# A two-block network on one core: norm weights moved from the rows to the transposed side, and the rms factor to what follows the projections

## Chip, core and metric

One Trainium2 core runs the whole kernel in one launch. The metric is the device time of one execution in microseconds (us). PE is the matrix engine, DVE the vector engine, ACT the scalar engine, POOL the GpSimd engine; SP only starts weight loads.

## What is computed

256 tokens of width 2048 pass through a first block (four branches merged by gates, an out-projection and a layer norm) and then a second one (an rms norm, a projection into a state-space group and a forget-gate attention, an out-projection, and a layer that selects among 16384 experts). What lies between the two blocks, and what reads it, is this:

```python
def layer_norm(x, g, b):
    ...
    y = (xf - mu) * lax.rsqrt(var + LN_EPS) * g.astype(jnp.float32) + b.astype(jnp.float32)
    return y.astype(x.dtype)

def first_block(x, w_in, ...):
        ...
        out = jnp.einsum('bsd,de->bse', merged, w_out[l])
        x = layer_norm(ALPHA * x + out, ln_g[l], ln_b[l])

def rmsnorm(x, w):
    xf = x.astype(jnp.float32)
    xf = xf * lax.rsqrt(jnp.mean(xf * xf, axis=-1, keepdims=True) + EPS)
    return (xf * w.astype(jnp.float32)).astype(x.dtype)

def second_block(x, ln1_w, w_in, ...):
        h = rmsnorm(x, ln1_w)
        proj = h @ w_in
        z, xbc, dt_raw, q, k, v, f_raw = jnp.split(proj, split_at, axis=-1)
        y_ssd = ssd_group(z, xbc, dt_raw, ...)
        y_fox = fox_group(q, k, v, f_raw, fox_f_bias)
        x = x + jnp.concatenate([y_ssd, y_fox], axis=-1) @ w_out
        x = x + peer(rmsnorm(x, ln2_w), peer_wq, peer_k1, peer_k2, peer_u, peer_v)
```

The layer norm's result is needed twice: normed, as the input of block 2's projection, and as it is, as the residual to which block 2's out-projection is added.

## The kernel before

**The stream.** All weights pass through as chunks of 128 x 2048 (1 MB), loaded by SP into three buffers `wr`. Each chunk is used in two halves of 128 x 1024. ACT casts a half into a rounded high part `wh`, DVE subtracts to get the low part `wl`, and there are four buffers of each. PE multiplies three times per 128 rows of the contraction: high part of the activations by `wh`, low part by `wh`, high part by `wl`. The activations stand transposed (width on partitions, tokens along the free side) in `XH` (high) and `XL` (low). `N_chunk` makes an output with tokens on partitions, by matmuls of 512 columns, six for each half and each token half t = 0, 1; `T_chunk` makes an output with tokens along the free side, by matmuls of 256 columns, 24 for each half.

**Order.** Each engine executes what the program wrote for it, in that order; there is no dynamic scheduling. The loop at the end of `_kern` walks over the halves. `catch` writes the cast and the subtraction of the halves up to three ahead (`LOOK`), then the half's matmuls are written, and after its first few matmuls `bg()` writes steps of background tasks (generators in four lanes). Which task steps come where is set by estimated clocks in `Tasks` and `Meter`, at build time. A task step that one engine has to wait for is therefore a wait for all that the same engine has behind it.

**The boundary between the blocks.** The rows `X[0]`, `X[1]` (128 tokens x 2048 each) hold block 1's sum. `state["tail"](t)` evicts the last 512 columns of the out-projection into them; `ln_stats` makes mean and standard deviation of the rows. Then `ln_part` and `ln_last` apply the layer norm in pieces of 128 x 512, with `lng` and `lnb`, the weights and offsets broadcast over all partitions, which were loaded into the buffers `GC` and `CV` during block 1; ACT squares the pieces and sums them, `rms_diag` makes a 128 x 128 diagonal matrix of 1/rms, and `to_T` multiplies pieces of X by it on PE, which transposes and scales at once (16 matmuls for each t), evicts with the rms norm's weight `ln1_w` to `XH` on ACT and `XL` on DVE. POOL takes the last piece of the layer norm and four `wl` subtractions.

PE's stream goes on meanwhile where it can. The first four chunks of block 2's `w_in2` (96 matmuls of 512 columns, for half of the attention's V) stand in the boundary: `N_chunk(..., lead=boundary1b)` writes the token half t = 0 of the first two chunks (24 matmuls), then calls `boundary1b`, which transposes t = 1, and writes the led t = 1 matmuls after it. Next come one chunk with 32 matmuls for dt and the forget gate (`dtf_chunk`; it has one cast, a small subtraction `wh<-wr,wh` and no `wl` for each half) and twelve `T_chunk`s for the state-space group's input (`ev_xbc` into `PX`). `ev_dtf` evicts the dtf output to `LS`, and `tr`, written two background points later, transposes it back by two PE instructions `pm<-cst,LS` in the middle of the second half of the first xbc chunk.

Of the kernel before, what the change touches and what calls it, by code (L numbers as in the profile page):

```python
# [16 lines left out]
P = 128  # L17
D = 2048
# [15 lines left out]
for _name, _w in (("pool_scale", 8), ("conv_w", 31 * 8), ("conv_b", 8), ("conv_g", 8), ("conv_lb", 8),  # L34
                  ("conv2_w", 48), ("conv2_b", 12), ("ln1_w", 16), ("ln2_w", 16), ("ssd_norm", 8)):
    PAR[_name] = (_n, _w)
    _n += _w
# [181 lines left out]
def _kern(tc, nc, ctx, A, out):  # L219
# [125 lines left out]
    def N_chunk(kq, evac, korder=(0, 1, 2, 3), hold=False, lead=None, slot=0):  # L345
        def fn(half, hi, lo):
# [456 lines left out]
    for br, (_, need, ysrc) in enumerate(order):  # L803
# [4 lines left out]
        for jj in range(8):  # L808
            def pre_y(need=need, ysrc=ysrc, br=br):
                flush()  # L810
                tasks.require(*need)
                if br == 0:
                    tasks.require("pool")
                split_Y(ysrc)
                if br == 2:
                    nc.gpsimd.dma_start(X[0], A["xN"][0])
                    nc.gpsimd.dma_start(X[1], A["xN"][1])
                    nc.gpsimd.dma_start(GC.rearrange("p j t -> p (j t)"), row_ap("ln_g"))
                if br == 3:
                    nc.gpsimd.dma_start(CV.rearrange("p j t -> p (j t)"), row_ap("ln_b"))  # L820
# [29 lines left out]
    def warm():  # L850
        SC.activation(small[:, 63:64], eps5, AF.Sqrt)

# [9 lines left out]
    diag = [per.tile([P, P], F32, name=f"diag{t}") for t in range(2)]  # L862
# [20 lines left out]
    lnb = CV.rearrange("p j t -> p (j t)")  # L883
    lng = GC.rearrange("p j t -> p (j t)")

# [8 lines left out]
    def ln_last(t):  # L894
        rs = small[:, 6 + t:7 + t]
        s = slice(1536, 2048)
        SC.activation(X[t][:, s], X[t][:, s], AF.Identity, bias=small[:, 8 + t:9 + t], scale=rs)
        G.tensor_tensor(X[t][:, s], X[t][:, s], lng[:, s], op=OP.mult)
        G.tensor_tensor(X[t][:, s], X[t][:, s], lnb[:, s], op=OP.add)

    def ln_part(t, hooks=()):
        mv = small[:, 2 * t:2 * t + 2]
        rs = small[:, 6 + t:7 + t]
        for h in (0, 1, 3, 2):
            s = slice(h * 512, (h + 1) * 512)
            if h < 3:
                V.scalar_tensor_tensor(X[t][:, s], X[t][:, s], mv[:, 0:1], lng[:, s], op0=OP.subtract, op1=OP.mult)
                V.scalar_tensor_tensor(X[t][:, s], X[t][:, s], rs, lnb[:, s], op0=OP.mult, op1=OP.add)
            SC.activation(VQ[:, s], X[t][:, s], AF.Square, accum_out=small[:, 16 + 4 * t + h:17 + 4 * t + h])
            if h < len(hooks):  # L910
                hooks[h]()
# [5 lines left out]
    def boundary1():  # L917
        flush()
        hc = tasks.now
        state["tail"](0)  # L920
        ln_stats(0)
        ln_last(0)
        ln_part(0, [lambda: catch(hc, G), lambda: catch(hc + 1, G)])
        state["tail"](1)
        rms_diag(0, sum_sq(0))
        ln_stats(1)
        to_T(0, "ln1_w", {2: lambda: catch(hc + 2, G), 6: lambda: catch(hc + 3, G), 10: lambda: ln_last(1)})
        ln_part(1)
        rms_diag(1, sum_sq(1))

    def boundary1b():
        to_T(1, "ln1_w")
        state["hold"] = False
        p1.close()
        block2()
# [5 lines left out]
    def block2():  # L941
# [36 lines left out]
        b2["sel"] = a2.tile([P, 32], BF, name="sel")  # L978
        V.memset(b2["c4"][:, :, 3], 0.0)
        with nc.allow_low_precision(reason="sums of an identity's entries"):  # L980
            V.tensor_reduce(b2["sel"], ident.rearrange("p (a h) -> p h a", a=4), axis=AX.X, op=OP.add)
        tasks.add("dt", dt_gen)
# [9 lines left out]

    def ev_dtf(o):
# [3 lines left out]
        def tr():  # L997
# [4 lines left out]
            V.tensor_tensor(b2["dtf"], p4[:, :, 0], b2["fb"][:, None, :].to_broadcast([P, 2, 32]), op=OP.add)  # L1002
            V.tensor_tensor(b2["dtf"], p4[:, :, 1], b2["dtf"], op=OP.add)
# [221 lines left out]
    def ev_k2(j):  # L1225
        def f(o):
            SC.copy(b2["K2"][:, j % 2], o)
            flags["k2"] = j + 1
        return f

    def ev_z(n):
        def f(t, ps):
            s = b2["w"].tile([P, 512], F32, name="t2")
            SC.activation(s, ps, AF.Sigmoid)
            V.tensor_tensor(b2["ZN"][:, t, n * 512:(n + 1) * 512], ps, s, op=OP.mult)
# [3 lines left out]
    def ev_vf(n):  # L1239
        def f(t, ps):  # L1240
            SC.copy(b2["VN"][:, t, n * 512:(n + 1) * 512], ps)
        return f

    def fox_gen(j):
        def make(ln):
# [18 lines left out]
            for blk in range(2):  # L1264
# [8 lines left out]
                for i in (1, 0):  # L1273
                    V.scalar_tensor_tensor(L[:, i, :nk], ps[i][:, :nk], 0.125,
# [33 lines left out]
               pres=[boundary1] + [None] * 3)  # L1308
# [425 lines left out]
def layout(inputs):  # L1734
# [56 lines left out]
    def tp(v):  # L1791
# [5 lines left out]
                                  tp(f["ssd_norm_w_2"])], axis=1)  # L1797
# [49 lines left out]
```

## Time and profile before

| what | value |
| --- | --- |
| median of 3 runs | 3078.73 us (3076.59 to 3081.01) |
| the profiled execution's own time | 3082.12 us |
| its span, first to last instruction | 3080.4 us |
| granted TensorE clock, mean over the span | 0.996 |
| PE busy | 3031.5 us (98%) |
| DVE, ACT, POOL busy | 2202.0, 1575.4, 214.6 us |

All times inside the kernel are those of one profiled execution, counted from its span's start. The boundary lies at 1112 to 1169 us of it, and block 2's projections and mixers end near 1460 us. A granted clock of 1.00 is 2.4 GHz, one of 0.50 is 1.2 GHz.

### The profile page before, as it was taken

To read this page: it belongs to the slowest core of one execution; us is meant where nothing else is said; L and a number is where in the kernel's file an instruction comes from. 1 tells how busy PE (TensorE), PEld (TensorE's weight loads), DVE (VectorE), ACT (ScalarE), POOL (GpSimd) and SP (SyncE) were. 2 spreads that over 40 slices of the span, in tenths; PEclk is the share of its full clock that TensorE was granted. 3 is DMA by queue.
4 is the path that set the end of the run, shared out by engine and by line. 5 is a ranking of instruction groups with operands and counts; after the bars stand their busy time and mean duration, and the time that the engine had idled before them with its cause. 6 is when DMAs were issued, how large, how long until landed. Compare 5 with 4: busy or idle time off the path is not lost.

```text
span 3080.4 us, 53114 instructions
## 1 busy us (share of the span) xinstructions
PE 3031.5 (98%) x21972; PEld 2829.0 (92%) x21972; DVE 2202.0 (71%) x3195; ACT 1575.4 (51%) x2199; POOL 214.6 (7%) x187
## 2 busy tenths in 40 slices
PE   8999999999999989999999999999999999999998
PEld 8899999999999869897799999999999888888887
DVE  7888866555555667665589989779796666666665
ACT  4443566444444445566444467667675444444444
POOL 0000000000000020100000012223131000000000
PEclk9999999999999999999999999999999999999999
DMA  7555455555555535433445565675658766666654
GB/s 267 193 185 192 177 199 180 210 196 209 192 205 193 192 127 187 165 137 137 178 178 192 207 218 208 244 264 213 248 194 344 269 245 221 247 251 250 240 212 150
DMA packets 92227, 640.61 MB, mean 208 GB/s; under 512 B 10273, under 2 KB 10449, under 8 KB 17745
## 3 DMA queue, kind: packets, MB, share of 16 engines
q1 hardware_dynamic: 78192, 559.06, 50.4%
q0 software_dynamic: 13504, 77.63, 6.9%
q8 instruction: 172, 2.82, 0.4%
q14 instruction: 71, 0.57, 0.1%
q10 hardware_dynamic: 288, 0.52, 0.0%
HBM read 601.53 MB, written 35.65 MB: 207 GB/s over the span
## 4 chain that ended last, share of the span: by engine, by line
PE 96%; DVE 1%; ACT 1%; issue 1%; DMA 0%; POOL 0%; SPq 0%; DVEq 0%; ACTq 0%
PE pm L208 92%; PE bg L208 4%; ACT wh L208 1%; DVE wl L208 0%; DMA wr<-w_in 0%; DVE X L208 0%; DVE XL L208 0%; POOL keys L1531 0%; DVE stg L208 0%; DVE gb L208 0%; ACT XH L208 0%; DVE PX L208 0%; ACT PX L208 0%; ACT keys L208 0%; SPq L433 0%
## 5 line engine op out<-in xcount | busy, mean ns | idle before, releaser
L208 DVE TENSOR_TENSOR wl<-wr,wh 128x1024 fp32r<-128x1024 f32 x1048 | 1292.4, 1236 | 804.6 <-ACT wh L208 799.5
L208 ACT CAST wh<-wr 128x1024 fp32r<-128x1024 f32 x1054 | 1109.2, 1053 | 1364.4 <-PE pm L208 1307.5
L208 PE MATMUL pm<-XH,wh 128*128 128x256 f32 x4976 | 1388.9, 279 | 8.0 <-ACT wh L208 8.0
L208 PE MATMUL pm<-XL,wh 128*128 128x256 f32 x4976 | 1379.0, 277 | 0.0
L208 PE MATMUL pm<-XH,wl 128*128 128x256 f32 x4960 | 1375.6, 277 | 1.1 <-DVE wl L208 1.1
L208 PEld LDWEIGHTS pm<-XH,wh 128*128 128x128 f32 x4976 | 936.2, 188 | 14.2 <-ACT wh L208 8.0
L208 PEld LDWEIGHTS pm<-XL,wh 128*128 128x128 f32 x4976 | 936.9, 188 | 1.0 <-issue 0.7
L208 PEld LDWEIGHTS pm<-XH,wl 128*128 128x128 f32 x4960 | 933.6, 188 | 1.6 <-DVE wl L208 1.6
L208 PE MATMUL pm<-wh,whl 128*128 128x512 f32 x1024 | 398.3, 389 | 0.0
L208 PE MATMUL pm<-wh,whh 128*128 128x512 f32 x1024 | 398.3, 389 | 0.0
L208 PE MATMUL pm<-wl,whh 128*128 128x512 f32 x1024 | 398.3, 389 | 0.0
L208 PEld LDWEIGHTS pm<-wl,whh 128*128 128x128 f32 x1024 | 192.3, 188 | 39.9
L208 PEld LDWEIGHTS pm<-wh,whh 128*128 128x128 f32 x1024 | 192.3, 188 | 39.8
L208 PEld LDWEIGHTS pm<-wh,whl 128*128 128x128 f32 x1024 | 192.3, 188 | 39.8
L208 PE MATMUL pm<-wh,XH 128*128 128x512 f32 x448 | 177.7, 397 | 3.7 <-ACT XH L208 3.7
L208 PE MATMUL pm<-wh,XL 128*128 128x512 f32 x448 | 176.8, 395 | 0.7 <-DVE XL L208 0.7
L208 PE MATMUL pm<-wl,XH 128*128 128x512 f32 x448 | 176.2, 393 | 0.0
L208 PE MATMUL pm<-YH,wh 128*128 128x256 f32 x512 | 141.9, 277 | 0.0
L1531 POOL TENSOR_TENSOR keys<-cst,t 128x512 f32<-128x512 f32 x64 | 126.9, 1983 | 211.2 <-ACT ga L208 211.0
L208 PE MATMUL pm<-YL,wh 128*128 128x256 f32 x512 | 141.5, 276 | 0.0
L208 PE MATMUL pm<-YH,wl 128*128 128x256 f32 x512 | 141.5, 276 | 0.0
L208 DVE SCALAR_TENSOR_TENSOR CV<-R,par,CV 128x256 f32<-128x256 f32 x240 | 116.2, 484 | 7.3
(292 smaller groups left out, 2368.5 us busy)
## 6 DMA issues: line engine op xcount, KB each, us to landing
wr<-w_in SPq DMA_DIRECT2D x190, 1024.0 KB, 4.8
wr<-uT SPq DMA_DIRECT2D x128, 1024.0 KB, 4.9
wr<-v SPq DMA_DIRECT2D x128, 1024.0 KB, 4.8
wr<-w_branch SPq DMA_DIRECT2D x32, 1024.0 KB, 4.8
wr<-w_out SPq DMA_DIRECT2D x32, 1024.0 KB, 4.8
wr<-wq SPq DMA_DIRECT2D x16, 1024.0 KB, 4.8
Ad<-ast POOLq DMA_DIRECT2D x16, 1024.0 KB, 5.1
Gd<-stg POOLq DMA_DIRECT2D x16, 1024.0 KB, 10.2
```

The source lines that it names most:

```text
L208: return f(out, *a, **k)
L1531: G.tensor_tensor(x, it, t3[:, 0, n0:n0 + 4, None].to_broadcast([P, 4, P]), op=OP.subtract)
```

## The change

The rows are only centred and scaled by the layer norm's mean and deviation (`normal`, on DVE or ACT). `turn` transposes a 128 x 512 piece on PE with the identity and evicts it on ACT with a scale and a bias per partition: `ln_g*ln1_w` and `ln_b*ln1_w`, which are made beforehand in `gb_w`; the result, in `VQ`, is rounded to `XH` and subtracted to `XL`. What is now multiplied by `w_in2` lacks the factor 1/rms of each token. A new background task, `resid`, makes the layer norm's true rows (times `ln_g`, plus `ln_b`), their squares, 1/rms as a column `rr` and, by one PE product of ones with diagonals, as a matrix `Rr` with tokens along the free side. Each eviction of block 2's projections multiplies by one of them; `tr` requires that `resid` is finished. The two broadcast rows are loaded no longer in block 1 but by POOL at the end of the boundary, into block 2's buffers `ZN` and `YF`. The diff, cut:

```diff
@@ N_chunk
                 if len(led) == 4:
-                    lead()
-                    for a in led:
+                    lead(-1)
+                    for n, a in enumerate(led):
                         part(*a)
+                        lead(n)
...
-                nc.gpsimd.dma_start(GC.rearrange("p j t -> p (j t)"), row_ap("ln_g"))
-                if br == 3:
-                    nc.gpsimd.dma_start(CV.rearrange("p j t -> p (j t)"), row_ap("ln_b"))
...
+        V.tensor_tensor(gb_w[:, 0], pv("ln_gT", 0, 16), pv("ln1_w", 0, 16), op=OP.mult)
+        V.tensor_tensor(gb_w[:, 1], pv("ln_bT", 0, 16), pv("ln1_w", 0, 16), op=OP.mult)
...
+    def normal(t, h, act=False):
+        x = X[t][:, h * 512:(h + 1) * 512]
+        rs = small[:, 6 + t:7 + t]
+        if act:
+            SC.activation(x, x, AF.Identity, bias=small[:, 8 + t:9 + t], scale=rs)
+        else:
+            V.tensor_scalar(x, x, small[:, 2 * t:2 * t + 1], rs, op0=OP.subtract, op1=OP.mult)
+    def turn(t, h, act=False):
...
+            PE.transpose(p[:, i * P:(i + 1) * P], X[t][:, k * P:(k + 1) * P], ident)
...
+            SC.activation(u[:, i * P:(i + 1) * P], p[:, i * P:(i + 1) * P], AF.Identity,
+                          bias=gb_w[:, 1, k:k + 1], scale=gb_w[:, 0, k:k + 1])
...
+        if act:
+            SC.copy(hs, u)
+        else:
+            V.tensor_copy(hs, u)
+        V.tensor_sub(XL[:, 4 * h:4 * h + 4, t * P:(t + 1) * P], u, hs.bitcast(F32))
@@ boundary1
-        ln_last(0)
-        ln_part(0, [lambda: catch(hc, G), lambda: catch(hc + 1, G)])
+        normal(0, 0)
+        normal(0, 1)
+        catch(hc)
+        turn(0, 0)
+        catch(hc + 1)
+        turn(0, 1, True)
         state["tail"](1)
-        rms_diag(0, sum_sq(0))
         ln_stats(1)
-        to_T(0, "ln1_w", {2: lambda: catch(hc + 2, G), 6: lambda: catch(hc + 3, G), 10: lambda: ln_last(1)})
-        ln_part(1)
-        rms_diag(1, sum_sq(1))
...
+    def boundary1b(n):
+        hc = tasks.now
+        if n < 0:
+            turn(1, 1, True)
+            normal(0, 2)
+            normal(0, 3)
+        elif n == 0:
+            turn(0, 2)
+            normal(1, 2)
+        elif n == 1:
+            catch(hc + 1)
+            turn(1, 2)
+            normal(1, 3)
+        elif n == 2:
+            catch(hc + 2)
+            turn(0, 3)
+        else:
+            turn(1, 3)
+            state["hold"] = False
+            p1.close()
+            block2()
@@ block2
+        nc.gpsimd.dma_start(b2["ZN"].rearrange("p t c -> p (t c)"), row_ap("ln_g"))
+        nc.gpsimd.dma_start(b2["YF"].rearrange("p j t -> p (j t)"), row_ap("ln_b"))
+    def resid_gen(ln):
...
+                V.tensor_tensor(X[t][:, s], X[t][:, s], g[:, s], op=OP.mult)
+                V.tensor_tensor(X[t][:, s], X[t][:, s], b[:, s], op=OP.add)
...
+                SC.activation(junk, X[t][:, s], AF.Square, accum_out=small[:, 16 + 4 * t + h:17 + 4 * t + h])
...
+            SC.activation(small[:, 10 + t:11 + t], sum_sq(t), AF.Sqrt, bias=eps6, scale=1.0 / D)
...
+        V.reciprocal(rr[:, :2], small[:, 10:12])
+        V.tensor_scalar(rr[:, 2:], rr[:, :2], 0.125, None, op0=OP.mult)
...
+            V.tensor_scalar(diag[t], ident, rr[:, t:t + 1], None, op0=OP.mult)
...
+            PE.matmul(p[:, t * P:(t + 1) * P], ones, diag[t], start=True, stop=True)
+        SC.copy(b2["Rr"], p[:, :S])
...
+            V.tensor_scalar(b2["VN"][:, t, :512], b2["VN"][:, t, :512], rr[:, t:t + 1], None, op0=OP.mult)
@@ ev_dtf, tr
-            V.tensor_tensor(b2["dtf"], p4[:, :, 0], b2["fb"][:, None, :].to_broadcast([P, 2, 32]), op=OP.add)
-            V.tensor_tensor(b2["dtf"], p4[:, :, 1], b2["dtf"], op=OP.add)
+            tasks.require("resid")
+            for c in range(2):
+                for i in range(2):
+                    V.scalar_tensor_tensor(b2["dtf"][:, c], p4[:, c, i], b2["rr"][:, c:c + 1],
+                                           b2["dtf"][:, c] if i else b2["fb"], op0=OP.mult, op1=OP.add)
@@ ev_xbc; ev_k2 likewise
-            SC.copy(b2["PX"][:, j, 3:], o)
+            V.tensor_tensor(b2["PX"][:, j, 3:], o, b2["Rr"], op=OP.mult)
...
-               pres=[boundary1] + [None] * 3)
+               pres=[(boundary1, boundary1_1), (boundary1_2, boundary1_3), None, None])
```

What is left out of it: `boundary1_1` to `boundary1_3` write two splits, `normal(1, 0)` and `normal(1, 1)` on ACT, and `turn(1, 0)`; the scales at the evictions of z, the second V half and the attention's scores take `rr` as an operand that the instruction already had room for.

The first place is DVE's order from the last `XL` of the boundary on. `wl<-wr,wh` and `wh<-wr,wh` are the stream's subtractions, X are the rows. Before:

```order
L208 MEMSET c_12620 128x2x32
L208 TENSOR_REDUCE sel<-cst 128x32
L208 TENSOR_TENSOR wl<-wr,wh 128x1024 x4
L208 TENSOR_TENSOR wh<-wr,wh 128x8x32 x2
L208 TENSOR_TENSOR wl<-wr,wh 128x1024 x5
L208 TENSOR_TENSOR dtf<-pm,fb 128x64
L208 TENSOR_TENSOR dtf<-pm,dtf 128x64
L208 TENSOR_TENSOR wl<-wr,wh 128x1024
```

And now, in the same place:

```order
L209 MEMSET c_12604 128x2x32
L209 TENSOR_REDUCE sel<-cst 128x32
L209 TENSOR_TENSOR wl<-wr,wh 128x1024 x2
L209 TENSOR_TENSOR wh<-wr,wh 128x8x32
L209 TENSOR_TENSOR X_76<-X_76,ZN 128x512
L209 TENSOR_TENSOR X_76<-X_76,YF 128x512
L209 TENSOR_TENSOR X_76<-X_76,ZN 128x512
L209 TENSOR_TENSOR X_76<-X_76,YF 128x512
L209 TENSOR_TENSOR wh<-wr,wh 128x8x32
L209 TENSOR_TENSOR wl<-wr,wh 128x1024 x2
L209 TENSOR_TENSOR X_76<-X_76,ZN 128x512
L209 TENSOR_TENSOR X_76<-X_76,YF 128x512
```

Products and sums of the rows now stand between the stream's subtractions; ten more of them, three `wl`, and the small steps to `rr`, `diag` and `VN` follow before the four steps that make `dtf`. So 16 operations on X with six of the stream's subtractions (the second `wh`, and five `wl`) lie between the arrival of `ZN` and the diagonal.

The second place is PE's order in the second half of the first xbc chunk, around the transposes of dtf (`pm<-cst,LS`). Before:

```order
L208 MATMUL pm<-XH,wl 128x256
L208 MATMUL pm<-cst,LS_12609 128x64 x2
L208 MATMUL pm<-XH,wh 128x256
L208 MATMUL pm<-XL,wh 128x256
L208 MATMUL pm<-XH,wl 128x256
```

And now:

```order
L209 MATMUL pm<-XH,wl 128x256
L209 MATMUL pm<-cst,LS_12593 128x64 x2
L209 MATMUL bg_12817<-diag,cst 128x128 x2
L209 MATMUL pm<-XH,wh 128x256
L209 MATMUL pm<-XL,wh 128x256
```

The two products with `diag` (fp32, into a bank `bg`) are new here, in front of the stream's next matmul; in both programs 161 stream matmuls stand between the out-projection's last one and this place (96 of `w_in2`'s first four chunks, 32 of dtf and 33 of xbc).

The third place is POOL's queue at the end of the boundary, with `fb`, `ea`, `ds` as small constants of block 2. Before:

```order
L898 TENSOR_TENSOR X_76<-X_76,GC 128x512
L899 TENSOR_TENSOR X_76<-X_76,CV 128x512
L297 TENSOR_TENSOR wl<-wr,wh 128x1024 x4
L898 TENSOR_TENSOR X_77<-X_77,GC 128x512
L899 TENSOR_TENSOR X_77<-X_77,CV 128x512
L970 DMA fb<-rows 128x32
L971 DMA ea<-rows 128x16
L972 DMA ds<-rows 128x16
L973 MEMSET PX 128x12x3
```

And now:

```order
L819 DMA X_77<-xN 128x2048
L1006 DMA fb<-rows 128x32
L1007 DMA ea<-rows 128x16
L1008 DMA ds<-rows 128x16
L1009 MEMSET PX 128x12x3
L1017 DMA ZN<-rows 128x2048
L1018 DMA YF<-rows 128x2048
```

POOL has no arithmetic left in the boundary, and two loads of 1 MB stand behind the small ones, whose first is held until the boundary's buffers are free.

## Rows read from the trace of the kernel before

**Rows 1.** Page: busy time of each engine, and the chain that ended last.
```profile
PE 3031.5 (98%) x21972; PEld 2829.0 (92%) x21972; DVE 2202.0 (71%) x3195; ACT 1575.4 (51%) x2199; POOL 214.6 (7%) x187
...
PE 96%; DVE 1%; ACT 1%; issue 1%; DMA 0%; POOL 0%; SPq 0%; DVEq 0%; ACTq 0%
```

**Rows 2.** Timeline of PE, 1108 to 1172: start, length, tile, idle before and releaser.
```profile
1112.09 0.39 PE L208 MATMUL pm<-wh,XL 128*128 128x512 f32 x1
1112.32 0.40 PE L208 MATMUL pm<-wl,XH 128*128 128x512 f32 x1
1122.34 4.46 PE L208 MATMUL bg<-diag,X 128*128 128x128 f32 x24 [9.63 <-issue]
1127.30 1.14 PE L208 MATMUL bg<-diag,X 128*128 128x128 f32 x8 [0.50 <-DVE XL L208]
...
1139.13 5.75 PE L208 MATMUL bg<-diag,X 128*128 128x128 f32 x32 [5.17 <-DVE diag L208]
...
1161.22 0.28 PE L208 MATMUL pm<-XH,wh 128*128 128x256 f32 x1
...
1168.96 0.39 PE L208 MATMUL pm<-XH,wh 128*128 128x256 f32 x1
```

**Rows 3.** Grouped instructions by form, 1106 to 1460: count; busy us, mean ns; idle before.
```profile
L208 DVE TENSOR_TENSOR wl<-wr,wh 128x1024 fp32r<-128x1024 f32 x93 | 113.6, 1224 | 92.3 <-ACT wh L208 88.4 <-PE bg L208 3.8
L208 ACT CAST wh<-wr 128x1024 fp32r<-128x1024 f32 x99 | 103.8, 1050 | 103.3 <-PE pm L208 82.2 <-issue 17.6 <-ACT LS L208 1.8
...
L208 ACT ACTIVATE VQ<-X 128x512 f32<-128x512 f32 x8 | 5.0, 627 | 10.1 <-DVE X L208 10.0
...
L208 DVE TENSOR_TENSOR XS<-XS,LS 128x256 f32<-128x256 f32 x12 | 4.9, 419 | 0.0
...
L208 ACT COPY PX<-pm 128x256 f32<-128x256 f32 x12 | 4.4, 365 | 0.0
...
L208 DVE TENSOR_TENSOR XL<-YF,XH 128x512 fp32r<-128x512 f32 x4 | 2.6, 684 | 0.0
...
L208 DVE TENSOR_SCALAR PX<-PX,ss 128x512 f32<-128x512 f32 x4 | 1.9, 487 | 0.1
...
L208 ACT ACTIVATE small<-small,eps 128x1 f32<-128x1 f32 x4 | 1.2, 294 | 8.0 <-DVE small L208 8.0
```

**Rows 4.** Timeline of PE, 1422 to 1456, columns as in rows 2.
```profile
1423.72 0.63 PE L208 MATMUL bg<-cst,PX 128*128 128x128 f32 x4 [2.02 <-DVE PX L208]
...
1451.02 0.80 PE L208 MATMUL pm<-wh,XH 128*128 128x512 f32 x1 [3.66 <-ACT XH L208]
```

**Rows 5.** Timeline of ACT, 1422 to 1456.
```profile
1424.97 1.13 ACT L208 ACTIVATE XS<-bg,par 128x128 f32<-128x128 f32 x4
```

**Rows 6.** Timeline of POOL, 1108 to 1172.
```profile
1138.93 0.59 POOL L970 DMA_DIRECT2D fb<-rows  x1 [5.16 <-ACT small L208]
1139.53 0.54 POOL L971 DMA_DIRECT2D ea<-rows  x1
...
1140.58 0.15 POOL L973 MEMSET PX<- 128x36 f32 x1
```

**Rows 7.** DMA issues: queue, count, KB each, median us from issue to landing.
```profile
CV<-rows POOLq DMA_DIRECT2D x1, 1024.0 KB, 4.9
```

**Rows 8.** Windows: length; busy PE, PEld, DVE, ACT, POOL; PEclk, DMA share, GB/s.
```profile
2881.00:2886.00 5.00, 5.00 (x24) 4.14 (x23) 2.12 (x2) 2.11 (x2) 0.00 (x0) 1.00 1.01 419
```

**Rows 9.** Windows of the boundaries and the first xbc projections, columns as rows 8.
```profile
1115.30:1125.60 10.30, 3.26 (x15) 3.29 (x16) 8.10 (x14) 4.64 (x12) 4.17 (x2) 0.50 0.29 103
...
1139.20:1142.60 3.40, 3.40 (x16) 3.40 (x17) 1.22 (x4) 1.82 (x6) 1.53 (x4) 0.51 0.37 9
...
1168.70:1235.00 66.30, 66.29 (x572) 65.98 (x572) 54.27 (x106) 34.60 (x58) 0.00 (x0) 1.00 0.51 176
...
1449.80:1456.70 6.90, 4.95 (x11) 3.57 (x12) 5.55 (x9) 2.63 (x4) 0.00 (x0) 0.51 0.57 177
```

More of the change, by code (lines that the diff above doesn't have):

```diff
@@ L860, in _kern @@
                    pres=[pre_wout if n == 0 else None, warm if n == 3 else None, None, None])
-    diag = [per.tile([P, P], F32, name=f"diag{t}") for t in range(2)]
+    diags = per.tile([P, 2, P], F32, name="diag")
+    diag = [diags[:, t] for t in range(2)]
+    gb_w = per.tile([P, 6, 16], F32, name="gb_w")
     def rms_diag(t, ss):
@@ L892, in ln_stats @@
         V.scalar_tensor_tensor(small[:, 8 + t:9 + t], mv[:, 0:1], -1.0, rs, op0=OP.mult, op1=OP.mult)
-    def ln_last(t):
+    def normal(t, h, act=False):
+        x = X[t][:, h * 512:(h + 1) * 512]
         rs = small[:, 6 + t:7 + t]
[L896 to L911, printed above, removed]
+        if act:
[3 more added lines that the diff above has]
+    def turn(t, h, act=False):
+        p = pA(h if t == 0 else (h + 2) % 4)
+        u = VQ[:, h * 512:(h + 1) * 512]
+        for i in range(4):
+            k = 4 * h + i
+            PE.transpose(p[:, i * P:(i + 1) * P], X[t][:, k * P:(k + 1) * P], ident)
+        for i in range(4):
+            k = 4 * h + i
+            SC.activation(u[:, i * P:(i + 1) * P], p[:, i * P:(i + 1) * P], AF.Identity,
+                          bias=gb_w[:, 1, k:k + 1], scale=gb_w[:, 0, k:k + 1])
+        u = u.rearrange("p (k t) -> p k t", k=4)
+        hs = XH[:, 4 * h:4 * h + 4, t * P:(t + 1) * P]
+        if act:
[3 more added lines that the diff above has]
+        V.tensor_sub(XL[:, 4 * h:4 * h + 4, t * P:(t + 1) * P], u, hs.bitcast(F32))
     def sum_sq(t):
@@ L921, in boundary1, with boundary1_1, boundary1_2, boundary1_3 @@
         ln_stats(0)
-        ln_last(0)
-        ln_part(0, [lambda: catch(hc, G), lambda: catch(hc + 1, G)])
+        normal(0, 0)
[4 more added lines that the diff above has]
+        turn(0, 1, True)
         state["tail"](1)
-        rms_diag(0, sum_sq(0))
         ln_stats(1)
-        to_T(0, "ln1_w", {2: lambda: catch(hc + 2, G), 6: lambda: catch(hc + 3, G), 10: lambda: ln_last(1)})
-        ln_part(1)
-        rms_diag(1, sum_sq(1))
[L931 to L935, printed above, removed]
+    def boundary1_1():
+        catch(tasks.now + 1)
+        normal(1, 0, True)
+        normal(1, 1, True)
+    def boundary1_2():
+        catch(tasks.now + 1)
+    def boundary1_3():
+        turn(1, 0, True)
+    def boundary1b(n):
[19 more added lines that the diff above has]
+            block2()
     p2 = ExitStack()
@@ L1240, in f @@
         def f(t, ps):
-            SC.copy(b2["VN"][:, t, n * 512:(n + 1) * 512], ps)
+            dst = b2["VN"][:, t, n * 512:(n + 1) * 512]
+            if n:
+                SC.activation(dst, ps, AF.Copy, scale=b2["rr"][:, t:t + 1])
+            else:
+                SC.copy(dst, ps)
+                flags["vf"] = t
         return f
```

39 lines of the change are left out of this document (31 added, 8 removed).

## The prediction

> **What bounds the kernel now.** I read the page first: PE is busy in 98% of the span and carries 96% of the chain that ended last [rows 1], so the time changes only by PE's waits, by the work in its queue, or by its clock. Next PE's timeline at the boundary, which shows where the stream stops. In what follows T is the time after 1112.7, where the last out-projection matmul ends. PE stands idle 9.63 + 0.50 + 5.17 = 15.3 us, and the three pieces of diagonal matmuls take 4.46 + 1.14 + 5.75 = 11.35 us [rows 2], so about 26 us pass without a stream matmul. The first 96 `w_in2` matmuls end at T = 48.5 (1161.2), and the stream goes on after the dtf transposes at T = 56.2 (1168.96) [rows 2]. That is the reference point: up to it both programs execute the same 161 stream matmuls. Last come the windows, for two facts. PE ran at half clock, 0.50 and 0.51, after the idle stretches, and in the 66 us after the boundary DVE is busy 54.27 of 66.30 us with PE 66.29 of 66.30 [rows 9]: DVE has little room there and PE none.
>
> **What the opening becomes.** The diagonal matmuls, squares and rms steps leave the path; eight `turn`s come. One `turn` is four transposes, 0.63 by the four at 1423.72 [rows 4]; four ACT evictions with scale, 1.13 [rows 5]; the rounding copy, on ACT 0.63 by the ACT pass over 128x512, on DVE not shown in that form: between 0.42 (half the columns) and 0.68 (a subtraction of that size) [rows 3], and I take 0.49, the row of a one-input operation of that size; and the subtraction, 0.68. `normal` costs 0.49 on DVE, 0.63 on ACT [rows 3]. Followed in the order written:
> - First two pieces of t = 0, with a cast between the evictions: 0.63 + 1.13 + 1.05 + 1.13 + 0.63 + 0.68, then the last out-projection piece of t = 1 on DVE, two operations of 0.68, and two small statistics steps of at most 0.29 each [rows 3]: T = 7.2.
> - Cast 1.05, two `normal`s on ACT 1.26, cast 1.05, its subtraction 1.22 and four matmuls at 0.23, the step between two starts [rows 2, 3]: T = 12.7.
> - `turn(1,1)` and a `normal`, 0.63 + 1.13 + 0.63 + 0.68 + 0.49: T = 16.3. `turn(0,2)` with the copy on DVE and a `normal`: 3.4, T = 19.7. The last three: 0.63 + 1.13 + 0.49 + 0.68 + 0.49, a subtraction of the stream 1.22, copy and subtraction of `turn(0,3)` 1.17, an eviction 1.13 and copy and subtraction of `turn(1,3)` 1.17: 8.1, T = 27.8.
>
> The led matmuls run between these, so PE has 48 left about T = 23.6 and ends the 96 near T = 34.6, 13.9 us earlier than before. This is what the change gains, if nothing else happened.
>
> **What the residual task costs.** The stream reaches the dtf transposes 7.7 us later (1161.2 to 1168.96 [rows 2]), at T = 42.3, and there meets the product with `diag`, behind which all its matmuls queue. When is `diag` ready?
> - POOL's `fb` waits for the last readers of block 1's buffers, now DVE's last `XL`: 0.5 of handover after T = 27.8, as PE's wait for DVE's `XL` at 1127.30 [rows 2], then 0.59 + 2 x 0.54 + 0.15 [rows 6] until `ln_g` is issued at T = 30.1, `ln_b` 0.54 later. One such load takes 4.9 us [rows 7], so alone `ln_b` lands at 35.5. But SP's next weight chunk is issued in the same microsecond. Three blocks of 1 MB at the 419 GB/s that the busiest window shows [rows 8] need 7.5 us, and 2.4 more is the part of 4.9 that isn't transport (4.9 less 1.05 MB at 419): T = 40.5. I take 39.0, near the shared bound.
> - From then DVE has 15 operations of 128x512 (one product needs `ln_g` alone): 15 x 0.68 = 10.2. Between them stand six subtractions of the stream, 0.42 + 5 x 1.2 = 6.4 [rows 3]. Two of these wait for a cast that stands on ACT behind two squares that wait for DVE: twice a square 0.63 and a cast 1.05, with the handovers 2.0 each, 4.0. At the end the last square 0.63, and sums, root, reciprocal, factor and diagonals, five steps of at most 0.29: 2.0 [rows 3]. Sum 22.6: `diag` at T = 61.6, and after two products, 0.5, PE goes on at T = 62.1.
>
> So PE waits near T = 43 to 61 (the last casts come late too, so this may be two waits) where it had waited at the opening, and resumes 62.1 - 56.2 = 5.9 us later.
>
> **The clock.** After idle stretches of 9.63, 5.17 and 3.66 us PE ran at half clock (1.2 GHz) for 3.3 us from 1122.34, for 3.4 from 1139.2 and for 5.7 from 1451.0 [rows 2, 4, 9]: half of it is lost, 1.6 to 2.8. In the kernel before these fell on transposing that DVE and ACT set the pace of; the new wait ends in the stream. I take 2.3 for it, and 1.0 more (0 to 2.8) for the opening, where the stops are short.
>
> The Trainium skill, "DMA: Bandwidth & Descriptors", section "Issuing engines are not separate DMA queues", says that transfers started from different engines land on the same 16 DMA engines and interleave. By it the shared bound holds, a sum of about +9; by the landing of 4.9 alone it would be about +5.7. No run so far shows two row loads beside a weight chunk.
>
> **What else moves.** Twelve evictions to `PX` (0.37 each on ACT) become DVE products of 0.42, and eight for K likewise [rows 3]: 5.0 and 3.4 us more DVE. In the window after the boundary DVE has 12 us spare of 66 [rows 9] and the subtractions are written up to three halves ahead, which hides them; without that cover they would cost their 5.0. The removed loads of block 1 and the two tiny products for `gb_w` lie beside idle time: POOL, which starts them, is busy for 7% of the span, and DVE for 71% [rows 1]. The two later waits of 2.02 and 3.66 [rows 4] depend on the task order, which shifts a little: between -3 and +5, and I take 0.
>
> **Sum.** 5.9 + 2.3 + 1.0 = +9.2 us. On the profiled execution's 3082.12 this gives 3091.3; the median of the runs, 3.4 lower, gives 3078.73 + 9.2 = **3088**.
>
> Bounds. Low: opening at 26, rows landing alone at 33.6, chain of 18.5 (no handover waits), resume at 52.6, clock 1.6, later waits -3: -5, thus 3073. High: opening 29, landing 42, chain 26 (twice the handovers), resume at 68.5 or +12.3, clock 4, later waits +3: about +19, thus 3098.
>
> **Rivals.**
> - *Rows land early and the handovers are short*: the same mechanism near its low end, landing 36, chain 20, resume at 56.5, +0.3, with a clock loss of 1.6 about +1: 3080. For it: ACT is busy only 34.60 of 66.30 us after the boundary [rows 9], so a cast should seldom wait. Against: the order ties casts to squares and squares to DVE.
> - *The residual task is hidden* (faster). If `diag` is ready by T = 42, PE doesn't wait; the 13.9 us stay, less about 1.5 for products and clock: -12.4, 3066. It decides from there: to be 6.2 us faster the stream must resume by T = 47 or so with the clock's loss. For it: the transposes end 13.9 us earlier. Against: 16.6 us of DVE work after a landing that can't come before about T = 33.6, so 50 at best; it needs the loads much earlier than the order in POOL's queue lets me see.
> - *The opening runs at half clock* (slower, by more). The new opening has short bursts of transposes between DVE and ACT steps. Before, PE was at 0.50 for 3.3 us while diagonal matmuls ran after a stop [rows 9]. If this holds through T = 0 to 34, the 96 matmuls take 0.23 more each for some 55 of them: +12.8 to the end of the 96. The wait for `diag` would then hide a part of it but the loads, which hang on the opening, come later too: about +12.8 in all, 3091.5.
>
> The Trainium skill's page "TensorE: Matmul & The Clock Gate", section "Part 4: PE-mode transpose", says that transposes done on PE don't count as work for its clock as matmuls do; it speaks for this last rival. The kernel before shows no boundary with transposes alone, so no row here agrees or disagrees yet.
>
> **How the numbers follow.** 0.2%, 6.2 us, is about what a measurement of this kernel can tell from no change (3072.6 to 3084.9). Forecast, +4 to +11 (3083 to 3090): 0.50. Early rows: 0.24. Hidden task: 0.13. Half clock in the opening: 0.13. The predicted time is the forecast's 3088. The range 3073 to 3098 leaves out the hidden task and a little above, under 2 in 10. Faster is the hidden task, 0.13. Same is the early rows, 0.24, and a small part of the forecast, 0.07: 0.31. Slower is the rest, 0.56.
>
> **What would show it.** In the profile after: `w_in2`'s 96 matmuls end near T = 35; DVE's first product X<-X,ZN starts only when ZN lands, T 35 to 39; PE waits at `bg<-diag,cst` for DVE's `diag`, 10 us or more in one wait or with one for `wh` or `wl` ahead of it; half clock after it; PX made by DVE without waits of PE for `wl`. I'm wrong if that wait is under 5 us (hidden task), if the stream resumes before T = 50, if the clock in the opening stays at 0.50 past T = 15, or if PE's waits for `wl` between 1170 and 1440 add up to over 5 us, in which case DVE has become the bound of the projections.

## The result, and the profile after

The changed kernel is slower: 3120.16 us median of 4 runs (3118.56 to 3120.38), against 3077.66 us for the kernel before (median of 4 runs, with one more than shown ahead). The ratio is 1.0136, with a 95% interval from 1.0124 to 1.0148: 42 us, where 9 were forecast. The profiled execution took 3120.03 us with a granted clock of 0.989. One of the ten executions of run 2 below took 5041.27 us at a granted clock of 0.563, and the ratios leave it out.

The page first, with the two rows that answer to [rows 1]:

```profile
PE 3042.2 (98%) x21944; PEld 2832.9 (91%) x21944; DVE 2213.6 (71%) x3218; ACT 1578.7 (51%) x2185; POOL 206.5 (7%) x179
...
PE 94%; DVE 2%; ACT 2%; DMA 1%; issue 1%; POOL 0%; SPq 0%; DVEq 0%; ACTq 0%
```

PE is still busy for 98% of the span, but its share of the chain fell from 96% to 94%, and DVE and ACT have 2% each instead of 1%. PE's busy time grew by 10.7 us (3042.2 less 3031.5) with nearly the same number of matmuls, at a mean granted clock of 0.989 instead of 0.996. The rest of the 38 us between the spans is waiting.

To see where, I compare the start of the same stream matmul in both traces. The last out-projection matmul starts at 1112.32 before and at 1107.26 after; these 5 us arise in the first 240 us of the program. They belong to the execution and not to the change: the runs below have both values whichever kernel they were made from (1107.5 in runs 2 and 3, which are the kernel before with small edits, 1112.5 and 1112.3 in runs 6 and 8, which are the changed kernel with edits). So all differences here are counted from that matmul:

| the same stream matmul, at its time before | what it is | after less before |
| --- | --- | --- |
| 1161.2 | the first of dtf, behind `w_in2`'s first 96 | -9.9 |
| 1169.0 | the first behind dtf's transposes | +11.8 |
| 1182.0 | when the clock is back | +14.4 |
| 1268.8 | ahead of the attention's heads | +13.5 |
| 1314.2 | after the first heads' K | +19.8 |
| 1363.6 | after the third forced chain (below) | +38.4 |
| 1468.0 | in block 2's out-projection | +42.6 |
| 3071.5 | the last one | +43.0 |

So there are four losses: 14.4 at the boundary (with the 9.9 won there spent), 6.3 at K, 18.6 in the attention's next heads, 4.2 around the second z chunk; 0.9 comes back between 1182 and 1268.8. From 1468 on nothing changes by more than half a microsecond.

**The boundary.** PE's timeline answers to [rows 2] (start, length, tile, idle before and releaser):

```profile
1107.26 0.40 PE L209 MATMUL pm<-wl,XH 128*128 128x512 f32 x1
...
1110.15 0.50 PE L209 MATMUL pm<-wh,XH 128*128 128x512 f32 x1 [1.62 <-DVE XH L209]
...
1116.29 0.79 PE L209 MATMUL pm<-wh,XH 128*128 128x512 f32 x1 [2.60 <-ACT wh L209]
...
1126.70 0.66 PE L209 MATMUL bg<-cst,X 128*128 128x128 f32 x4 [1.81 <-DVE X L209]
...
1130.61 0.66 PE L209 MATMUL bg<-cst,X 128*128 128x128 f32 x4 [1.86 <-DVE X L209]
...
1146.29 0.28 PE L209 MATMUL pm<-XH,wh 128*128 128x256 f32 x1
...
1156.82 0.58 PE L209 MATMUL pm<-XH,wh 128*128 128x256 f32 x1 [8.48 <-DVE wh L209]
...
1165.32 0.34 PE L209 MATMUL pm<-cst,LS 64*128 64x64 f32 x2 [1.17 <-ACT LS L209]
1174.88 1.22 PE L209 MATMUL bg<-diag,cst 128*128 128x128 f32 x4 [9.22 <-DVE diag L209]
```

With T counted from the end of the last out-projection matmul (1107.7), the 96 matmuls end at T = 38.6, before at 48.5. Then PE waits 8.48 us for the second small subtraction `wh` of dtf, and 9.22 for `diag`. DVE's timeline says why:

```profile
1138.82 0.69 DVE L209 TENSOR_TENSOR XL<-VQ,XH 128x512 fp32r<-128x512 f32 x1
...
1149.12 0.69 DVE L209 TENSOR_TENSOR X<-X,ZN 128x512 f32<-128x512 f32 x1 [6.56 <-DMA ZN<-rows]
1152.59 0.69 DVE L209 TENSOR_TENSOR X<-X,YF 128x512 f32<-128x512 f32 x1 [2.78 <-DMA YF<-rows]
...
1174.55 0.48 DVE L209 TENSOR_SCALAR diag<-cst,rr 128x128 f32<-128x128 f32 x2
```

The boundary's last `XL` starts at 1138.82 (T = 31.2, ends at 31.9); the first product of the residual task starts when `ZN` lands (T = 41.4), the first sum when `YF` does (44.9), and `diag` at T = 66.9. The landing of the two rows, in the view of the DMA issues, answers to [rows 7]:

```profile
ZN<-rows POOLq DMA_DIRECT2D x1, 1024.0 KB, 7.3
YF<-rows POOLq DMA_DIRECT2D x1, 1024.0 KB, 10.2
```

They took 7.3 and 10.2 us, where the same load took 4.9 in block 1. The Trainium skill, "DMA: Bandwidth & Descriptors", section "Issuing engines are not separate DMA queues", which says that such transfers interleave on the same DMA engines, is borne out: the shared bound worked out from [rows 7, 8] was 9.9 from the second issue.

The windows give the clock (columns as in [rows 8]); the second answers to the last of [rows 9], and the third holds one of the attention's stops:

```profile
1115.90:1120.90 5.00, 4.57 (x12) 3.26 (x13) 2.45 (x2) 3.08 (x6) 0.00 (x0) 0.50 0.11 25
1174.80:1181.30 6.50, 6.42 (x33) 6.42 (x34) 2.94 (x9) 3.32 (x6) 0.00 (x0) 0.56 0.00 0
1339.00:1352.20 13.20, 9.64 (x68) 8.37 (x67) 5.68 (x14) 6.45 (x18) 0.03 (x1) 0.87 0.24 81
```

PE ran at half clock for 5 us in the opening, behind waits of 1.62 and 2.60 us, and again behind the wait for `diag`. Behind the waits of 1.81 and 1.86 us it didn't.

**The attention.** PE's waits from 1182 to 1400 (us in total, how often, the longest), and below them all that the kernel before has from 1169 to 1400:

```profile
PE bg L209 <- DVE LS L209: 8.2, 3, 2.7
PE bg L209 <- DVE K L209: 4.9, 2, 3.4
PE bg L209 <- ACT LS L209: 1.4, 3, 0.5
PE bg L209 <- ACT YF L209: 1.1, 3, 0.4
...
PE bg L208 <- ACT K L208: 1.2, 2, 0.9
```

The three waits for `LS` and those for ACT behind them are three copies of one place. Its timeline, with the stream's cast and subtraction:

```profile
1339.40 1.04 ACT L209 CAST wh<-wr 128x1024 fp32r<-128x1024 f32 x1 [2.69 <-PE pm L209]
1340.35 0.40 ACT L209 ACTIVATE LS<-LS,smf 128x128 f32<-128x128 f32 x1
1340.47 1.22 DVE L209 TENSOR_TENSOR wl<-wr,wh 128x1024 fp32r<-128x1024 f32 x1 [1.30 <-ACT wh L209]
...
1342.15 0.53 PE L209 MATMUL bg<-cst,LS 128*128 128x128 f32 x2 [2.73 <-DVE LS L209]
...
1343.14 0.44 PE L209 MATMUL bg<-LS,VN 128*64 128x128 f32 x4 [0.46 <-ACT LS L209]
...
1343.94 0.48 PE L209 MATMUL bg<-K,q 64*128 64x256 f32 x1 [0.37 <-ACT YF L209]
```

PE waits 2.73 us for the head's softmax, then 0.46 for the copy of its transpose, then 0.37 for the copy of its result. Between these waits PE has none of the stream's matmuls: all steps of one head stand back to back. They are written so by `ev_q2`, which evicts q of head j into one of two buffers and so first calls `tasks.until` for head j - 2. `until` writes the steps of that head, one after the other, until its reading of q is written. Counted while the programs are built, the steps that `until` or `require` had to write are:

| kernel | at `resid` | at q of head 2 | 4 | 5 | 6 | 7 | second z chunk |
| --- | --- | --- | --- | --- | --- | --- | --- |
| before | no such task | 1 | 1 | 1 | 0 | 1 | 1 |
| after | 15 | 1 | 5 | 4 | 5 | 1 | 1 |

One such step costs nothing that shows; a run of four or five does: in the three chains PE waits 10.7 of the 18.6 us lost there, and part of the rest is half clock behind them. And the same table has the 15 steps of the residual task that `tr` requires.

**K.** The next lines are from the place of PE's wait of 3.4 us, with the clock behind it last:

```profile
1278.05 4.12 POOL L1204 TENSOR_TENSOR PX<-xsN,ds 128x1024 f32<-128x1024 f32 x2 [18.18 <-issue]
...
1280.28 2.97 DVE L209 TENSOR_TENSOR wl<-wr,wh 128x1024 fp32r<-128x1024 f32 x1 [1.73 <-ACT wh L209]
1283.18 0.41 DVE L209 TENSOR_TENSOR K<-pm,diag 128x256 f32<-128x256 f32 x1
...
1283.73 0.55 PE L209 MATMUL bg<-K,q 64*128 64x128 f32 x1 [3.40 <-DVE K L209]
...
1283.90:1290.00 6.10, 6.10 (x31) 5.78 (x32) 2.27 (x5) 2.13 (x2) 0.00 (x0) 0.52 0.49 172
```

The eviction of K stands on DVE behind a `wl` that took 2.97 us instead of 1.23 while POOL multiplied `PX`; before, ACT evicted K. The second wait, 1.5 us, stands behind a `wl` of the usual 1.23. The Trainium skill, "SBUF — State Buffer", section "Terms", says that DVE and GpSimd take turns for one pair of ports, and that who doesn't have it is blocked for the whole instruction of the other; this row agrees. So does the kernel before, where DVE came first: its `wl` took 1.23 us, and POOL's two pieces 5.42 us together instead of 4.12.

```profile
1257.22 5.42 POOL L1127 TENSOR_TENSOR PX<-xsN,ds 128x1024 f32<-128x1024 f32 x2 [12.07 <-issue]
...
1259.65 1.23 DVE L208 TENSOR_TENSOR wl<-wr,wh 128x1024 fp32r<-128x1024 f32 x1 [1.72 <-ACT wh L208]
```

**The second z chunk.** The loss there sits at the first of the two waits of [rows 4], PE's wait for `PX`, now 3.36 us instead of 2.02. Behind it PE ran at half clock; before, it did not (the last line is the kernel before):

```profile
1458.15 1.08 PE L209 MATMUL bg<-cst,PX 128*128 128x128 f32 x4 [3.36 <-DVE PX L209]
...
1458.10:1464.10 6.00, 5.95 (x17) 4.82 (x18) 1.93 (x4) 2.19 (x5) 0.00 (x0) 0.53 0.55 205
...
1423.70:1429.70 6.00, 5.97 (x28) 4.96 (x29) 3.53 (x7) 4.17 (x9) 0.00 (x0) 1.00 0.37 122
```

`PX` came later by the order on DVE: four small steps of a head's softmax, which stood ahead of the product `PX<-PX,ZN` before, now stand between it and the scaling `PX<-PX,ss` that PE waits for.

### The profile page after: what moved, and what is told of

The parts are those of the page before. It is cut to its first block, busy times and chain, and to the rows that moved or that the text cites. A ratio compares the mean times of both kernels' runs of the same rounds, so it can differ in the third digit from the quotient of the medians.

```text
span 3118.3 us, 53065 instructions
## 1 busy us (share of the span) xinstructions
PE 3042.2 (98%) x21944; PEld 2832.9 (91%) x21944; DVE 2213.6 (71%) x3218; ACT 1578.7 (51%) x2185; POOL 206.5 (7%) x179
## 4 chain that ended last, share of the span: by engine, by line
PE 94%; DVE 2%; ACT 2%; DMA 1%; issue 1%; POOL 0%; SPq 0%; DVEq 0%; ACTq 0%
PE pm L209 91%; PE bg L209 4%; DVE wl L209 1%; ACT wh L209 1%; DVE X L209 0%; DMA wr<-w_in 0%; DMA YF<-rows 0%; DVE XL L209 0%; ACT VQ L209 0%; POOL keys L1614 0%; DVE PX L209 0%; ACT t L209 0%; ACT PX L209 0%; DVE stg L209 0%; DVE ZN L209 0%
## 5 line engine op out<-in xcount | busy, mean ns | idle before, releaser
L1614 POOL TENSOR_TENSOR keys<-cst,t 128x512 f32<-128x512 f32 x64 | 135.7, 2120 | 211.2 <-ACT ga L209 211.0
```

The lines of the kernel that those rows point to most:

```text
L1614: G.tensor_tensor(x, it, t3[:, 0, n0:n0 + 4, None].to_broadcast([P, 4, P]), op=OP.subtract)
```

## The experiments

My first theory after the result, **forced steps**: the residual task takes the first of four lanes and DVE time in the estimated clocks, all later tasks are written later, and the stream's buffers force them out in runs. Rivals: **DVE evictions** (PX and K on DVE cost the time), **landing** (late rows hold the boundary), and later **the opening itself loses**. Times are medians; ratios are to the kernel before on the same chip, which took 3077 to 3080 us on the chips used, so that a difference between times of two chips holds to some 3 us. "In the trace" means the difference of the same stream matmul against the kernel before, as in the table above.

**1. Three buffers for q and K.**

```diff
-            if j >= 2 and ("fq", j - 2) not in flags:
-                tasks.until(f"fox{j - 2}", lambda: ("fq", j - 2) in flags)
-            t = b2["w"].tile([P, S], F32, name="q2")
+            if j >= 3 and ("fq", j - 3) not in flags:
+                tasks.until(f"fox{j - 3}", lambda: ("fq", j - 3) in flags)
+            t = b2["w"].tile([P, S], F32, name="q2", bufs=3)
```

> The changed kernel with three buffers instead of two for the attention's q and K, so that a q eviction looks three heads back and not two before it makes the program write out a head's remaining steps at once. Theory 'forced steps': three places in the changed kernel where such steps stand back to back on PE (waits 2.7 + 0.5 + 0.4 us and half clock behind each, about 6 us a place) vanish, some of it returns before the second z chunk: 12 to 18 us faster than the changed kernel, 3102 to 3108. Rival 'DVE evictions': the time goes because PX and K are now evicted by DVE; then at most 3 us faster, 3117 or more.

Measured: 3103.02 us, ratio 1.0077 [1.0060, 1.0094], 17 us less than the changed kernel. No wait for `LS` is left from 1182 to 1400, and in the trace the three chains cost nothing (16.2 us behind before them, 14.4 after them). A part returns before the second z chunk, where the program now writes six steps of the last heads at once; PE's waits from 1400 to 1500 show them in one:

```profile
PE bg L209 <- DVE LS L209: 7.3, 1, 7.3
```

**2. The same in the kernel before.** The edit is the same, with K's plain copy.

> Control: the kernel before with the same three buffers. There each look back forces a single step and PE shows no wait for it, so both theories expect the time of the kernel before within 3 us, 3075 to 3081.

Measured: 3082.66 us, ratio 1.0010 [1.0000, 1.0020]: within the 3 us expected of the kernel before on this chip (3079.81), though above the range given in figures. The buffers by themselves gain nothing; what they gain in 1 is the change's own loss.

**3. The order alone.** The kernel before, with an empty task that only charges the estimated clocks:

```diff
+    def plan_gen(ln):
+        yield WAIT
+        for t in range(2):
+            for h in range(4):
+                tasks.charge("dve", 0.612)
+                tasks.charge("dve", 0.612)
+                yield GO
+                tasks.charge("act", 0.586)
+                yield GO
...
+        tasks.add("resid", plan_gen)
...
+            tasks.require("resid")
...
-            SC.copy(b2["PX"][:, j, 3:], o)
+            nc.scalar.copy(b2["PX"][:, j, 3:], o)
+            tasks.charge("dve", 0.346)
```

> The kernel before with all its own work, only the order in which background tasks are written is that of the changed kernel: an empty task in the place of the residual task charges the estimated clocks with the same costs, dtf's transposes require it, and the evictions to PX and K stay on ACT but are charged to DVE. 'Forced steps' expects the same forced chains in the attention: 15 to 22 us slower than before, 3093 to 3100, waits of PE for DVE's LS near 2.7 us. 'DVE evictions', where the work itself costs the time, expects no more than 3 us from the kernel before.

Measured: 3093.11 us, ratio 1.0044 [1.0027, 1.0061]: 13 us slower than before, with the same instructions in another order. Its waits from 1182 to 1400 are those of the changed kernel to the tenth:

```profile
PE bg L208 <- DVE LS L208: 8.2, 3, 2.7
PE bg L208 <- ACT LS L208: 1.4, 3, 0.5
PE bg L208 <- ACT YF L208: 1.1, 3, 0.4
```

The program has 5, 5 and 5 forced steps at the same three heads. So order alone makes the three chains; they cost 20.6 us in the trace, and some 6 us are won at other places. This is the run that decides between order and work. It doesn't part the residual task's charges from those of the evictions to `PX` and K, which it moves too.

**4. Early rows.** `ln_g` and `ln_b` loaded in block 1 into `GC` and `CV`, which now outlive it and serve as `ZN` and `YF`:

```diff
+    p12 = ExitStack()
+    a12 = p12.enter_context(tc.tile_pool(name="a12", bufs=1))
+    CV = a12.tile([P, 8, S], F32, name="CV")
+    GC = a12.tile([P, 8, S], F32, name="GC")
...
-        b2["YF"] = a2.tile([P, 8, S], F32, name="YF")
+        b2["YF"] = CV
...
-        nc.gpsimd.dma_start(b2["ZN"].rearrange("p t c -> p (t c)"), row_ap("ln_g"))
-        nc.gpsimd.dma_start(b2["YF"].rearrange("p j t -> p (j t)"), row_ap("ln_b"))
```

> The changed kernel with the broadcast ln_g and ln_b loaded during block 1, into two buffers that outlive it and become ZN and YF. Theory 'landing sets the residual task': DVE's waits for the two rows (6.6 and 2.8 us) vanish and the stream resumes 8 to 10 us earlier at dtf, 3109 to 3113. Rival 'casts and squares set it': DVE's waits come back as waits between the stream's casts and the squares, gain under 3 us, 3117 or more. The rest of block 2 is the same in both.

Measured: 3106.52 us, ratio 1.0085 [1.0068, 1.0101]. In the trace the stream passes dtf's transposes 10.0 us earlier than in the changed kernel (+1.8 instead of +11.8), about the 6.6 and 2.8 us of DVE's two waits for rows. The times fell by 13.6, more than the 8 to 10 expected; the trace has 10.3 of it. PE's waits at the boundary:

```profile
PE bg L209 <- DVE diag L209: 9.2, 1, 9.2
...
PE pm L209 <- ACT LS L209: 1.8, 1, 1.8
```

The wait for `wh` is gone, but that for `diag` is what it was, 9.2 us. So the landing sets when the residual task starts, and the wait for `diag` is the task's own end: the 15 steps that `require` writes at once, the products, sums and squares of t = 1 and the steps to `diag`, one behind the other, while PE's next matmuls stand behind them.

**5. PX and K on ACT, with the order kept** (the factor 1/rms is left out of them):

```diff
-            V.tensor_tensor(b2["K2"][:, j % 2], o, b2["Rr"], op=OP.mult)
+            nc.scalar.copy(b2["K2"][:, j % 2], o)
+            tasks.charge("dve", 0.346)
```

> The changed kernel with PX and K evicted by a plain ACT copy as before, so the 1/rms factor is left out of xbc and k; the order of the background tasks is kept (the clocks are still charged as for DVE). Theory 'DVE evictions cost about 8 us': PE's waits for K (3.4 and 1.5 us) and their half clock vanish, 3111 to 3115. Rival 'only the order costs': within 3 us of the changed kernel, 3117 to 3123.

Measured: 3115.24 us, ratio 1.0115 [1.0099, 1.0132]. The runs alone hardly tell 5 us from none (the two intervals overlap); the traces do: the waits for K are 0.2 us instead of 4.9 (first line below), and the stream loses nothing from 1268.8 to 1314.2 (12.1 to 11.6 us behind) where the changed kernel loses 6.3. The three forced chains stay, 8.2 us of waits for `LS`. So K's eviction is a cost of its own, of 6 us; PX's shows none.

```profile
PE bg L209 <- ACT K L1305: 0.2, 1, 0.2
PE bg L209 <- DVE LS L209: 8.2, 3, 2.7
```

**6. Rows and buffers together** (edits 1 and 4).

> The changed kernel with both the early rows and the three buffers of q and K. If the two costs are separate (one at dtf, one in the attention) the gains of 13.6 and 17 us add: 3089, between 3086 and 3093. Rival 'the attention is late because the boundary is late', so that the early rows had already taken a part of the forced steps away: 3097 or more.

Measured: 3090.68 us, ratio 1.0037 [1.0023, 1.0051]. The two gains add.

**7. No forced residual task.** On top of 6, dtf's transposes move into the `dt` task, which waits for `resid` without writing it; PX and K are evicted by ACT and multiplied later:

```diff
+        yield from wait_done("resid")
...
+            PE.transpose(p[:, i * 64:(i + 1) * 64], t[:64, i * P:(i + 1) * P], ident[:64, :64])
...
-            tasks.require("resid")
...
+                yield from wait_done("resid")
+                V.tensor_tensor(PX[:, j, 3:], PX[:, j, 3:], b2["Rr"], op=OP.mult)
```

> The kernel with early rows and three buffers, in which dtf's transposes no longer require the residual task: they become the first step of the dt task, which is only taken up when the residual task is done; PX and K are evicted by ACT as before and multiplied by 1/rms in a step of their own (PX on DVE in the convolution task, K on POOL). Theory 'the wait for diag is a forced chain': PE's 9.2 us wait and its half clock vanish and nothing takes its place, 11 us faster than with rows and buffers alone. Rival 'the residual task's DVE and ACT work has to go somewhere': the tasks behind it slip and the attention's steps are forced again in spite of three buffers, no more than 3 us gained, or a loss.

Measured: 3109.07 us, ratio 1.0095 [1.0079, 1.0112], 18 us slower than 6. The rival holds. The wait for `diag` did vanish, and the stream runs ahead: 10.2 us ahead of the kernel before at 1182, and 21.2 at 1324.7. Then the attention takes it all back: forced runs of 2, 5, 8, 8 and 5 steps at five heads, and PE's waits from 1182 to 1400 are

```profile
PE bg L209 <- DVE LS L209: 15.5, 4, 5.8
PE bg L209 <- ACT RB L209: 3.1, 2, 1.5
```

At 1468 the stream is 32 us behind. PE being early is worth nothing here while the background tasks are late.

**8. No residual work.** 1/rms set to one, rows left only centred and scaled, so that neither the residual's products, sums and squares nor the rms norm are computed:

```diff
+        rr = b2["rr"]
+        V.memset(rr[:, :2], 1.0)
+        V.memset(rr[:, 2:], 0.125)
+        V.memset(b2["Rr"], 1.0)
```

> The changed kernel with the residual task's rows, squares, 1/rms and products left out (1/rms is set to one, and the rows stay only centred and scaled). What is left is the opening, the POOL loads and the DVE evictions. Theory 'the opening gains 10 to 14 us and the residual task loses it': the stream passes dtf's transposes 10 to 14 us earlier than in the kernel before, and the whole is 3078 to 3090 with some forced steps left. Rival 'the opening itself loses (clock and short bursts)': dtf no earlier than before, 3095 or more.

Measured: 3092.98 us, ratio 1.0043 [1.0027, 1.0060]. The stream passes dtf 9.5 us earlier than before, so the opening does gain (the 10 to 14 expected were a little high). Yet the whole is 13 us slower than before, and above the 3078 to 3090 expected: tasks are forced even without the residual task's work (3, 3, 2 and 3 steps), K costs its part, and the waits from 1182 to 1400 name both:

```profile
PE bg L209 <- DVE K L209: 5.9, 2, 4.4
PE bg L209 <- ACT LS L209: 3.5, 3, 1.2
```

**9. The opening alone:** 8 with three buffers and PX and K on ACT, without a factor.

> What is left of the change when all three suspected costs are out: the residual task's work left out as in the run without it (1/rms set to one, rows only centred and scaled), three buffers of q and K, and PX and K evicted by plain ACT copies. If the three costs are all there is, only the opening's gain of 10 to 12 us remains: 3066 to 3072. Rival 'the background tasks bound block 2', so that a stream which runs ahead of them waits for them at the z and out-projection chunks: 3077 or more, no faster than before.

Measured: 3073.22 us, ratio 0.9981 [0.9971, 0.9991]. Between the two expectations: of the 9.7 us by which the stream passes dtf earlier, 9.2 are left at 1398.7 (times of the kernel before, as in the table), and in the trace 2 at 1468; the runs say 4 to 6. The rival of this run has a part in it even here. Most of what is lost goes at two waits between 1400 and 1500, with half clock behind each: one for a background task, one for block 2's out-projection, which was 3.66 in the kernel before [rows 4]:

```profile
PE pm L209 <- ACT XH L209: 4.7, 1, 4.7
PE bg L209 <- DVE LS L209: 1.7, 1, 1.7
```

This is what the idea brought here with the rms factor and the residual's rows at no cost at all: some 5 us.

**10. A whole version with the costs removed as far as I could:** 6, with K evicted by ACT and multiplied on POOL.

```diff
-            V.tensor_tensor(b2["K3"][j % 3], o, b2["Rr"], op=OP.mult)
+            SC.copy(b2["K3"][j % 3], o)
+            G.tensor_tensor(b2["K3"][j % 3], b2["K3"][j % 3], b2["Rr"], op=OP.mult)
```

> A whole computation: early rows and three buffers as in the run with both, and K evicted by ACT and multiplied by 1/rms on POOL, so that PE doesn't wait for DVE's K. Its part of the DVE evictions (waits of 3.4 and 1.5 us and half clock) should go: 5 to 7 us faster than with rows and buffers alone, 3083 to 3086, still slower than before by the wait for diag (9.2 us) and the forced steps ahead of the second z chunk. Rival 'POOL's product slows DVE and comes later': 3089 or more.

Measured: 3091.76 us, ratio 1.0038 [1.0024, 1.0053], no better than 6. POOL's first product stands behind POOL's own `PX` multiplication, and PE waits for POOL instead of DVE:

```profile
PE bg L209 <- POOL K L1308: 5.2, 2, 3.6
```

No version here beats the kernel before with the whole computation.

## Why the prediction was wrong

**The step that failed** is "What else moves": "The two later waits of 2.02 and 3.66 depend on the task order, which shifts a little: between -3 and +5, and I take 0." These two waits did stay in that range: the first lost some 4 us with its half clock, the second grew by 0.2 (3.9 instead of 3.66). What failed is what the sentence takes for granted, that the order could move time at these two waits only. It made new waits in the attention's heads, three chains that the sum has at nothing, and they cost 18.6 us; with the 6.3 at K, also at nothing, they are most of the 28.6 lost behind the boundary (43.0 less 14.4). I had read what the moved work costs on its engines, but not what it does to the order in which all later tasks are written. The order of the heads was there to be read before the run: a head's transposes `bg<-cst,LS`, its products with V and its next scores stand next to each other in it at these places, with nothing of the stream between, and the code has `until` in `ev_q2`. Runs 1 and 3 show this cause from both sides: with a third buffer the chains go, and with the order alone they come. Run 7 shows that the one cure tried by waiting more cleverly does not help; that the tasks come late there because the residual one takes DVE and ACT time is argued and not shown, and run 8 has forced steps without that work.

**The DVE evictions.** I had put K's and PX's twelve and eight products at 0 "which hides them", with 5.0 as the price without cover. For PX that was right: no wait of PE for `wl` or PX appears from 1182 to 1270. For K it was wrong, but not by DVE's load over the stretch: two of the eight evictions stood behind a `wl`, one of them stretched to 2.97 us beside POOL's work, and PE waited 4.9 us for them and ran at half clock behind the first, 6.3 us in all. Run 5 shows it.

**The boundary**, point by point (T after the last out-projection matmul):

| step | forecast | measured |
| --- | --- | --- |
| last `XL` | 27.8 | 31.9 |
| end of the 96 `w_in2` matmuls | 34.6 | 38.6 |
| second row lands | 39.0 | 44.9 |
| from there to the end of the wait for `diag` | 22.6 | 22.3 |
| stream resumes after dtf, against before | +5.9 | +11.8 |
| half clock behind the wait | 2.3 | 2.6 |

The mechanism was right: the opening gains, the residual task takes it back behind the landing, and the clock adds to it. Two terms of the sum were too small. The opening was 4 us longer, as an eviction of four pieces with scale and bias took 1.51 us and not the 1.13 of [rows 5], which has a scale alone, eight times, and 5 us of it ran at half clock. And the landing followed the shared bound (10.2 us from the issue; 9.9 by the bound, 8.4 by the value I took). The chain of the residual task I had right to 0.3 us, and not by luck: DVE's three waits for casts within it, 1.72, 0.52 and 1.79, add up to the 4.0 forecast. Run 4 bears it out, with the landing gone and the stream 10.0 us earlier. The signs listed in the prediction came, those with a time 2 to 4 us late; none of them looked past the boundary except PE's waits for `wl`.

**The rivals.** "Rows land early" and "hidden task" did not happen; run 4 brings the first about, and there the stream is 3.6 us late at 1182. "Half clock in the opening" happened for 5.0 us (window 1115.9 to 1120.9), not for 34: with stream matmuls between the transposes the clock came back. The sentence of the Trainium skill's page "TensorE: Matmul & The Clock Gate", section "Part 4: PE-mode transpose", on transposes alone was not put to the test by this. My tell-tale for "DVE has become the bound of the projections", waits for `wl`, stayed silent, as it should; I had none for waits at the background tasks.

What stays open: which charges delay the heads' steps, those of the residual task or those of the evictions moved to DVE, as no run has the one without the other and all else the same; and whether another placing of the residual task would have kept the opening's gain, of which run 7 tried one.

## What to carry to other kernels

Where background work is written between a stream's instructions by estimated costs, a new task changes more than its own time: compare the order of the tasks behind it, and count the places where a buffer or a `require` forces steps out back to back, for a run of four or five such steps cost PE 3.6 us of waits here, and half clock behind them. Look past the stage that the change was made for: two thirds of this loss lie behind it. A wait removed at the head of a stage is worth only as much as the work that ends the stage comes earlier (run 7). Moving an operation to another engine should be checked against what that engine shares a port with, not only against its busy time.

## What the runs showed of the hardware

- A DVE subtraction of 128x1024 took 2.97 us instead of 1.23 when a POOL product of 128x1024 had started first; in the kernel before, DVE came first and took 1.23, and POOL's two products took 5.42 instead of 4.12.
- A broadcast row of 1 MB took 4.9 us to land in block 1, 7.3 and 10.2 beside another one and a weight chunk.
- Four evictions of 128x128 from a PSUM bank on ACT took 1.51 us with a scale and a bias for each partition, eight times in the opening; with a scale alone they took 1.13 [rows 5].
- Behind waits of 1.62 and 2.60 us, with stream matmuls between them, PE ran at half clock (1.2 GHz) for 5.0 us. Behind a wait of 3.36 us it ran at 0.53 for 6.0 us, behind one of 2.02 at 1.00.
